# Weight loads of a hybrid-heads network's projections, issued from ScalarE's queue instead of SyncE's

## The chip, the cores and the metric

The kernel runs on one core of a Trainium2 chip. The metric is the device time of one execution in microseconds (us), lower is better. An engine executes its own instructions in the order in which they stand in the program; SyncE (SP) does nothing but issue transfers and wait.

## The reference, cut to what matters

Two layers of a network work on 512 latent and 256 context tokens of 2048 channels, all in 32-bit floats. Each layer modulates the normalised input, applies one large input projection, feeds four kinds of heads (a diagonal state space model "S5", windowed attention, bidirectional RWKV-7, Hyena convolutions), gates their outputs and applies an output projection:

```python
for l in range(DEPTH):                       # DEPTH = 2, D_MODEL = 2048
    mod_x = silu(c) @ w_ada[l] + b_ada[l]    # shift, scale, gate; the same for the context
    hx = rms_norm(x, norm_g[l]) * (1.0 + scale_x) + shift_x
    s5u, q, k, v, rkv, lora, hy, g = split_proj(hx @ w_in[l])
    y = concat(rms_norm(s5(s5u)), rms_norm(attention(q, k, v)), rwkv(rkv, lora), rms_norm(hyena(hy)))
    x = x + gate_x * ((y * silu(g)) @ w_out[l])
```

The context runs through the same weights; after the second layer only the latent tokens are wanted.

## The kernel before

Tiles have 128 partitions (channels) and up to 768 tokens (512 latent, 256 context). The input projection of a layer has 51 output tiles of 128 channels; each is computed in four parts (`kq` in `inprojs`, L1621), and a part uses one weight tile `wr` of 128x512 (256 KB). That is 408 loads from `in_win` over both layers. The output projection (`outproj`, L1716) has 16 output tiles with four such parts, 128 loads from `in_wo`.

A weight tile goes through three steps. `raw` (L1477) gives one of `WRB` = 3 buffers `wr`, and SyncE issues the load (L1629 or L1725). `split` (L1480) makes two parts of it: ScalarE (ACT) copies it to the rounded type, `wh` (L1484), and VectorE (DVE), or GpSimd (POOL) for every fourth part, subtracts that from the original, `wl` (L1485). `WHB` = 2 buffers of `wh` and `wl` exist. TensorE (PE) then multiplies: 12 matmuls of 512 columns and, where the context is wanted, 12 of 256 for each part (L1645, L1735). A buffer `wr` is free again when `wh` and `wl` have been made; a buffer `wh` when the part's matmuls are done.

Beside the input projection runs the modulation of later use: 64 blocks of `w_ada` (`ada_block`), four loads each (L1540, issued by SyncE) into the same three `wr` buffers, each read by four small matmuls (L1542). While these blocks run (to 2730 us), loads of `in_win` and of `in_wada` take the three buffers in turn. A few other loads (L248, L256, L1028) use them too.

The heads run at the same time as the projection. The one that matters below is RWKV: 24 groups of chunks, 12 in each layer, each of which goes round features (VectorE), an inversion on GpSimd (L398, L399: 62 instructions), with transfers ahead of it (`rwAd`, `rwAb`) and behind it (`rwXd` L401, `rwXP` L402), and a chain of small matmuls with ScalarE and VectorE between them (L439 to L466; `rwKU`, L448, is ScalarE's link). S5 loads 512 small tables (`s5T`, L807). All transfers of the kernel, 2575, are issued by SyncE.

A scheduler lays down the order of every engine when the kernel is built: it takes instructions by priority as they become ready on its own clock. `prio(WP)` gives loads and splits a priority 2000 instructions ahead of their place. At run time nothing is reordered: an instruction whose data are late holds all that stand behind it on its engine.

Of the kernel before, what the change touches and what calls it, by code (L numbers as in the profile page):

```python
# [37 lines left out]
# columns of the packed RWKV parameters  # L38
# [15 lines left out]
def pack_rw(I):  # L54
    f = [cols(I["rw_mu_prev"]), cols(I["rw_mu_next"]), cols(I["rw_w0"].reshape(2, -1)), cols(I["rw_a0"].reshape(2, -1)),
         cols(I["rw_k_k"]), cols(I["rw_k_a"]), cols(I["rw_r_k"].reshape(2, -1)), cols(I["rw_ln_g"]), cols(I["rw_ln_b"])]
    p = np.concatenate(f, axis=2)
    for o in (RP["mup"], RP["mun"]):
        p[:, :, o + 12] = p[:, LORA_ORDER, o + 12]
    wa = np.stack([I["rw_w2"], I["rw_a2"]], axis=2)  # layer, direction, (w, a), row, output  # L60
    return {"rwp": p, "rwwa": np.ascontiguousarray(wa.reshape(2, 4, 32, 512))}


class K:
# [26 lines left out]
    def padded(self, lat, ctx):  # L91
        """Copies a projection tile beside zeros; its used width with the last zero excluded."""
# [8 lines left out]
    @contextmanager  # L101
    def prio(self, offset):
        """Work that goes before what was traced up to offset instructions earlier."""
        self.tc.cur_priority -= offset
        yield
        self.tc.cur_priority += offset
# [9 lines left out]
    def ring(self, shape=(128, 512)):  # L116
        """The banks beside those of the input projection, in turn."""
# [3 lines left out]
    def rms(self, y, sq, tmp, eng, eps, gate=None):  # L121
        """1 / sqrt(mean square + eps) over 4 channel tiles y, in sq (all of one width). With gate, which runs beside it: half of that, from 4 eps."""
# [19 lines left out]
class Pace:  # L142
    """Issue order on the tensor engine: units of a filling stream issue behind steps of a leading one."""
# [4 lines left out]
    def step(self, ins, allow):  # L148
        """ins leads; the units that come before it grow by allow."""
        self.n += allow  # L150
        self.steps.append((self.n, ins.ins.name))
# [18 lines left out]
class RwFeed:  # L170
    """Token shift of the RWKV projections; r, k, kk, v and the half logits kept in both orders of time."""

    def __init__(self, k, l, raw):
# [5 lines left out]
        # 1 - mu_prev - mu_next, w0 / 2, a0 / 2, k_a / 2, 1 - k_a, 2 - k_a  # L179
# [11 lines left out]
        # r, k, kk, v and tanh of the half logits (decay, a), forward and reversed  # L191
# [7 lines left out]
    def store(self, d, z, ctx):  # L199
        """z [128, 769] (latent | - | context) into d [128, 2, NT], as it is and reversed."""  # L200
# [8 lines left out]
    def feed(self, j, lat, ctx):  # L209
        """Projection tile j (r 0-3, k 4-7, v 8-11, lora 12) in lat / ctx [128, n]: token shift."""  # L210
# [30 lines left out]
    def logits(self, lz):  # L241
        """tanh of half the decay and a logits of all channels: (high, low, high, low) x (high, high, low, low) in one product. In 8 parts."""
# [30 lines left out]
class Rwkv:  # L273
    """Bidirectional RWKV-7 over chunks of 64 steps; both directions advance together, each in its own order of time."""
# [13 lines left out]
    def features(self, c, g):  # L288
        """Scores and transposed operands of 4 chunks of two heads."""
# [6 lines left out]
        S = t([128, 2, 4, 2, 128], "rwS", self.nbuf)  # direction, (pair, head), parity  # L296
        KU = t([128, 2, 2, 2, 2, 128], "rwKU", self.nbuf)  # direction, pair, parity, (K/B | V/U)
# [28 lines left out]
        # slots of a pair: K even | B even | B odd | K odd, in the place of k and kk  # L326
# [17 lines left out]
        # end-scaled K (natural), B (chunks of a pair exchanged)  # L344
# [25 lines left out]
    def rows(self, b):  # L370
        """Partitions of the B rows and of the K rows of chunks of parity b."""
# [5 lines left out]
    def invert(self, S, XT):  # L377
        """Transposed inverses of the unit triangular scores; column 4 m + g of matrix u on partition 4 u + g."""
# [10 lines left out]
        grp = [(b, q, self.rows(b)[0].start + 32 * q) for b in (1, 0) for q in range(2)]  # by rising row  # L389
# [13 lines left out]
        # natural order of the columns; a row block is used from its diagonal on  # L403
# [3 lines left out]
        # off-diagonal block of the inverse: -X1^T A21^T X2^T  # L407
# [81 lines left out]
    def finish(self, c, Y, n0, out):  # L489
        """Head norm and bonus of the tokens from n0 on, in Y."""  # L490
# [5 lines left out]
        for a in range(n0, n0 + n, 256):  # L496
# [5 lines left out]
            # bonus: r k (2 - k_a + k_a (a forward + a backward)) summed over a head  # L502
# [73 lines left out]
def pack_s5(I):  # L576
    def st(a):  # [L,2,G,P] -> [L,128,2*G] with both halves alike
# [4 lines left out]
    lam = np.stack([st(I["s5_lam_re"]), st(I["s5_lam_im"]), stp], axis=2)  # [L,128,3,64]  # L582

    def bt(a):  # [L,2,G,P,H] -> [L,P,2G,H]
# [5 lines left out]
    bs = np.stack([np.concatenate([br, bi], 1), np.concatenate([bi, br], 1)], axis=2)  # [L,128,2,64,16]  # L590
# [7 lines left out]
class S5:  # L598
    """Bidirectional diagonal state space model over chunks of 8 tokens."""
# [7 lines left out]
    def turns(self, out, x, tmp, eng):  # L607
        """out = x - round(x)"""
# [3 lines left out]
    def prepare(self):  # L612
# [33 lines left out]
        # turns per chunk  # L646
# [6 lines left out]
        # powers 0..8 of lambda  # L653
# [18 lines left out]
        # (lambda - 1) / lam  # L672
# [15 lines left out]
        # BA = [re; im], BB = [-im; re] of the discretised input matrix  # L688
# [11 lines left out]
        # CA = [cr; -ci], CB = [-ci; -cr]  # L700
# [15 lines left out]
    def tile(self, ct, src):  # L716
        """Channel tile ct (8 groups); src [128, 768] in DRAM."""
# [6 lines left out]
        Uc = t([96, 8, 8, 16], "s5Uc")  # chunk | group, 7 - s, h  # L724
# [7 lines left out]
        U = t([128, 8, 128], "s5U")  # (7 - s, h) | group, chunks ctx, lat, ctx  # L732
# [6 lines left out]
        Yc = t([96, 8, 8, 16], "s5Uc")  # chunk | t, group, o  # L739
# [12 lines left out]
    def batch(self, g0, U, Yc):  # L752
        """Two groups, both directions."""
# [4 lines left out]
        def dg(a):  # [128, 64, ..] -> [128, 2, 2, ..]  # L758
# [7 lines left out]
        for d in range(2):  # L766
# [7 lines left out]
            # outputs at step t: forward lambda^(t+1), backward lambda^(8-t)  # L774
# [13 lines left out]
        # impulse response within a chunk: K_j[o, h] with h on partitions  # L788
# [20 lines left out]
        # drive matrices with (7 - s, h) on partitions: re | im | re  # L809
# [7 lines left out]
        # rotation tables  # L817
# [11 lines left out]
        # drives, rotated: v cos + [im; -re] sin  # L829
# [9 lines left out]
        # x: sin with the sign of [+; -]  # L839
# [6 lines left out]
        # rotated back, one chunk later, chunks in natural order lat | ctx  # L846
# [21 lines left out]
    def glu(self, outs, bg, eps):  # L868
        """Gated linear unit, then the branch norm."""
# [45 lines left out]
def hy_const(ns=(512, 256)):  # L915
    c = {}
    f = np.float32
    for n in ns:
# [6 lines left out]
        # taps: even, then odd  # L925
        h = n // 2
        ms = np.arange(n).reshape(h // 128, 128, 2).transpose(1, 2, 0)  # [128, parity, tile]
        c[f"hydec{n}"] = np.exp(-t * deltas[None, :]).astype(f)[ms].reshape(128, n // 128, 512).copy()
        # frequencies k below n / 2 (even, then odd) carry those of n - 1 - k too
# [7 lines left out]
        # [128 taps, frequency tile, cos / sin, parity, tap tile, 128]  # L937
        c[f"hykt{n}"] = kt.reshape(128, 2, 2, h // 128, h // 128, 128).transpose(0, 4, 1, 2, 3, 5).astype(f).copy()
        od = base % 2 == 1
        kk = np.concatenate([np.where(od, n - 1 - base, base), np.where(od, base, n - 1 - base)])  # even, then odd  # L940
        w = np.pi * (kk + 0.5) / n
        tau = np.arange(h)[:, None] + 0.5
        p, q = np.cos(tau * w) + np.sin(tau * w), np.cos(tau * w) - np.sin(tau * w)  # [h, n]
        # forward: a -> P even, b -> M even, b -> P odd, a -> M odd
        fw = np.stack([p[:, :h], q[:, :h], p[:, h:], q[:, h:]])  # [4, h, h]
        c[f"hyfw{n}"] = fw.reshape(4, h // 128, 128, h).transpose(2, 0, 1, 3).astype(f).copy()  # [128 t, 4, tt, k]
        c[f"hyiv{n}"] = fw.transpose(0, 2, 1).reshape(4, h // 128, 128, h).transpose(2, 0, 1, 3).astype(f).copy()  # [128 k, 4, kt, t]
# [18 lines left out]
class HyFilter:  # L966
    """Spectra of the filters. raw, split: buffers of 2 KB and their split."""
# [12 lines left out]
    def angle(self, ps, b, f, n):  # L980
        """f (ps + b) brought to the range of the sine."""
# [10 lines left out]
    def hidden(self, l, n):  # L992
        """The two layers with sines, transposed: high parts over low parts."""
# [24 lines left out]
    def tables(self, n):  # L1018
# [4 lines left out]
        self.tb = [t([128, 2, 2, 4, 128], f"hftb{i}", 1, F32R) for i in range(2)]  # frequency tile, cos / sin, (parity, taps)  # L1023
# [8 lines left out]
    def spectra(self, l, f, out):  # L1032
        """In 4 parts; appends the spectra of both orders to out."""
# [3 lines left out]
        for o in range(2):  # L1037
            # frequency tiles even then odd; [cos, sin] spectra scaled by 1 / (2 n)
# [7 lines left out]
            for s in (1, 0):  # L1046
# [4 lines left out]
                for par in range(2):  # L1051
                    S = []
                    for mt in range(h):
# [6 lines left out]
                        if par + mt == 0:  # L1060
                            # the backward filter has no tap at 0: half of sum and difference
# [29 lines left out]
class HyFeed:  # L1091
    """Convolution over 3 tokens of the projections."""
# [7 lines left out]
    def feed(self, j, lat, ctx):  # L1100
        """Projection tile j (v 0-3, x1 4-7, x2 8-11): convolution over 3 tokens."""
# [10 lines left out]
class Hyena:  # L1112
# [8 lines left out]
    def seq(self, n0, n, G):  # L1121
# [11 lines left out]
        for o in range(2):  # L1133
            # folded inputs, time on partitions
# [11 lines left out]
            # spectra P, M; products  # L1146
# [20 lines left out]
            for c in range(4):  # L1167
# [3 lines left out]
                # even P and odd M are even about the middle, the others odd  # L1171
# [16 lines left out]
    def finish(self, gates, bg, eps, put):  # L1188
        """Branch norm and gates; put takes the tiles."""
# [18 lines left out]
def att_const():  # L1208
# [5 lines left out]
    pm = np.zeros((128, 128), f)  # [source, destination]  # L1214
# [20 lines left out]
class KvFeed:  # L1235
    """RMS norm of queries and keys over heads of 64 channels."""
# [6 lines left out]
    def feed(self, gi, dram, lat, ctx):  # L1243
        """One tile of queries (gi 0) or keys (1)."""
# [16 lines left out]
class Attn:  # L1261
    """Windowed grouped-query attention with sinks; latent and context queries."""
# [16 lines left out]
    def rotate(self, x):  # L1279
        """Rotary embedding of the latent tokens."""  # L1280
# [8 lines left out]
    def run(self, srcs, pool):  # L1289
        """srcs: q 0-3, k, v. The results stay in pool."""  # L1290
# [6 lines left out]
        # keys of a group, both halves alike: high and low parts  # L1297
# [19 lines left out]
        def load(c):  # L1317
# [4 lines left out]
            # first head: high over low parts; second head: low over high parts  # L1322
# [25 lines left out]
    def finish(self, gates, outs, bg):  # L1348
        """Branch norm and gates."""
# [597 lines left out]
```

## Time and profile before

| | |
|---|---|
| Time, median of 3 runs | 3715.77 us (3714.04 to 3724.52) |
| Span of the profiled execution | 3742.2 us; no separate time of that execution is given |
| Profiled span against the median | 26.4 us or 0.7% longer |
| PE busy | 3482.5 us, 93% of the span |
| DVE, ACT, POOL busy | 60%, 40%, 37% |
| Granted TensorE clock, mean | 0.952 of full speed |
| Bytes moved by transfers | 515.12 MB, 138 GB/s over the span |

The profile's rows are of one execution. A wait row says which instruction waited for which, the total in us, how often and the longest. "Busy" leaves out issuing and waiting; so all of SyncE is waiting or issuing, and a wait there costs something only if what stands behind it is wanted sooner.

### The profile page before, as it was taken

To read this page: it belongs to the slowest core of one execution; us is meant where nothing else is said; L and a number is where in the kernel's file an instruction comes from. 1 tells how busy PE (TensorE), PEld (TensorE's weight loads), DVE (VectorE), ACT (ScalarE), POOL (GpSimd) and SP (SyncE) were. 2 spreads that over 40 slices of the span, in tenths; PEclk is the share of its full clock that TensorE was granted. 3 is DMA by queue.
4 is the path that set the end of the run, shared out by engine and by line. 5 is a ranking of instruction groups with operands and counts; after the bars stand their busy time and mean duration, and the time that the engine had idled before them with its cause. 6 is when DMAs were issued, how large, how long until landed. Compare 5 with 4: busy or idle time off the path is not lost. (4 is left out here: it accounts for less than half of the span.)

```text
span 3742.2 us, 63165 instructions
## 1 busy us (share of the span) xinstructions
PE 3482.5 (93%) x23222; PEld 2692.6 (72%) x23222; DVE 2234.8 (60%) x4239; ACT 1491.1 (40%) x2875; POOL 1386.2 (37%) x2508
## 2 busy tenths in 40 slices
PE   5897899999999999999999978999999999999999
PEld 1465777777778777788777866776776767677867
DVE  7673666546555544366667664775466565546765
ACT  3344433434344433244313454443434443435522
POOL 5642664152435242000143424663434455411031
PEclk9998999999999999999999988999988998999999
DMA  7855344554445444543633325435533433435244
GB/s 241 273 174 157 106 115 126 174 159 112 138 133 144 134 135 132 160 129 113 216 113 101 111 86 151 130 102 170 171 89 109 123 99 112 120 119 185 66 158 121
DMA packets 546737, 515.12 MB, mean 138 GB/s; under 512 B 166425, under 2 KB 392506, under 8 KB 545532
## 3 DMA queue, kind: packets, MB, share of 16 engines
q1 hardware_dynamic: 546428, 511.08, 45.2%
q8 instruction: 184, 3.01, 0.3%
q14 instruction: 125, 1.02, 0.1%
HBM read 406.59 MB, written 100.93 MB: 136 GB/s over the span
## 5 line engine op out<-in xcount | busy, mean ns | idle before, releaser
L1645 PE MATMUL pin<-hxh,wh 128*128 128x512 f32 (+1 forms) x2624 | 988.9, 377 | 10.6 <-ACT ev L267 5.0
L1645 PE MATMUL pin<-hxh,wl 128*128 128x512 f32 (+1 forms) x2624 | 946.2, 363 | 13.7 <-POOL wl L1485 10.0
L1645 PE MATMUL pin<-hxl,wh 128*128 128x512 f32 (+1 forms) x2624 | 945.8, 361 | 0.0
L1484 ACT ACTIVATE wh<-wr 128x512 fp32r<-128x512 f32 x548 | 344.4, 629 | 828.3 <-PE pin L1645 389.5
L1645 PEld LDWEIGHTS pin<-hxh,wh 128*128 128x128 f32 x2624 | 506.7, 193 | 126.7 <-issue 32.3
L1645 PEld LDWEIGHTS pin<-hxh,wl 128*128 128x128 f32 x2624 | 505.5, 193 | 96.1 <-POOL wl L1485 12.9
L1645 PEld LDWEIGHTS pin<-hxl,wh 128*128 128x128 f32 x2624 | 508.1, 194 | 73.3 <-issue 5.3
L1485 DVE TENSOR_TENSOR wl<-wr,wh 128x512 fp32r<-128x512 f32 x434 | 318.6, 734 | 306.7 <-ACT wh L1484 290.1
L1485 POOL TENSOR_TENSOR wl<-wr,wh 128x512 fp32r<-128x512 f32 x114 | 159.0, 1395 | 868.9 <-ACT wh L1484 755.5
L398 POOL TENSOR_TENSOR rwtm<-rwAb,rwX 128x60 f32<-128x60 f32 (+24 forms) x744 | 258.2, 347 | 343.9 <-DMA rwAb<-rwAd 148.1
L1735 PE MATMUL pin<-yh,wl 128*128 128x512 f32 (+1 forms) x768 | 281.5, 368 | 6.5 <-DVE wl L1485 6.4
L1735 PE MATMUL pin<-yh,wh 128*128 128x512 f32 (+1 forms) x768 | 281.8, 368 | 3.5 <-ACT yh L1711 1.3
L399 POOL TENSOR_TENSOR rwX<-rwX,rwtm 128x60 f32<-128x60 f32 (+24 forms) x744 | 263.1, 354 | 57.4
L1735 PE MATMUL pin<-yl,wh 128*128 128x512 f32 (+1 forms) x768 | 280.5, 365 | 2.3 <-DVE yl L1712 2.0
L1735 PEld LDWEIGHTS pin<-yh,wl 128*128 128x128 f32 x768 | 145.9, 190 | 32.3 <-DVE wl L1485 9.7
L1735 PEld LDWEIGHTS pin<-yh,wh 128*128 128x128 f32 x768 | 145.9, 190 | 30.1 <-ACT yh L1711 3.8
L1735 PEld LDWEIGHTS pin<-yl,wh 128*128 128x128 f32 x768 | 146.2, 190 | 26.7 <-DVE yl L1712 3.4
L1739 DVE SCALAR_TENSOR_TENSOR xt<-pin,GT,xt 128x512 f32<-128x512 f32 (+1 forms) x144 | 93.8, 656 | 87.0 <-PE pin L1735 86.7
L1542 PE MATMUL pin<-wr,cs 128*32 128x128 f32 x2048 | 119.8, 290 | 15.5 <-DMA wr<-in_wada 11.7
L448 ACT ACTIVATE rwKU<-mU 64x256 f32<-64x256 f32 x96 | 36.2, 377 | 194.4 <-PE mU L446 193.4
L466 DVE TENSOR_TENSOR rwst<-rwst,mU 64x128 f32<-64x128 f32 x160 | 45.3, 283 | 87.4 <-PE mU L459 84.6
L340 PE MATMUL mA<-rwZR,rwld 64*128 64x128 f32 x768 | 91.7, 288 | 5.5 <-DVE rwS L342 4.5
(608 smaller groups left out, 6548.7 us busy)
## 6 DMA issues: line engine op xcount, KB each, us to landing
wr<-in_win SPq DMA_DIRECT2D x408, 256.0 KB
wr<-in_wada SPq DMA_DIRECT2D x256, 256.0 KB
ada<-in_wada SPq DMA_DIRECT2D x64, 512.0 KB
wr<-in_wo SPq DMA_DIRECT2D x128, 256.0 KB
rwld<-rwF SPq DMA_DIRECT2D x20, 1024.0 KB
rwF<-ev SPq DMA_DIRECT2D x64, 256.0 KB
xt<-in_xin SPq DMA_DIRECT2D x32, 384.0 KB
rwLA<-ev SPq DMA_DIRECT2D x32, 384.0 KB
```

What stands on the lines that cost most here:

```text
L340: nc.tensor.matmul(pss[:, p, b, :], kb[hr, d * 2 + p, 2 * b:2 * b + 2, :].rearrange("p b s -> p (b s)"), ZR[hr, d, :, tt * 64:tt * 64 + 64 ...
L398: E.tensor_tensor(tm, Ab[:, 0:s, s:s + 1].to_broadcast([128, s, w]), X[:, s:s + 1, m:8].to_broadcast([128, s, w]), ALU.mult)
L399: E.tensor_tensor(X[:, 0:s, m:8], X[:, 0:s, m:8], tm, ALU.subtract)
L448: nc.scalar.activation(KU[rB, :, p, b, 1, :], up[rB].rearrange("p d a b -> p d (a b)"), AF.Copy, scale=-1.0)
L466: V.tensor_tensor(new[hs, :, hs], new[hs, :, hs], sp[hs], ALU.add)
L1484: nc.scalar.activation(h, raw, AF.Copy)
L1485: (nc.gpsimd if i % 4 == 3 else nc.vector).tensor_tensor(l, raw, h.bitcast(F32), ALU.subtract)
L1542: nc.tensor.matmul(ps[32 * j:32 * j + 32, :], self.cs[:, q * 4 + j, :], w3[:, j], start=q == 0, stop=q == 3, tile_position=(0, 32 * j))
L1645: mm.append(nc.tensor.matmul(ps, w[:, c], x[:, t], start=a, stop=b))
L1735: nc.tensor.matmul(ps, w[:, c], y[:, t], start=a, stop=b)
L1739: nc.vector.scalar_tensor_tensor(x[:, t], ps, self.GT[l][:, s, j:j + 1], x[:, t], ALU.mult, ALU.add)
```

## The change

A new method issues the weight loads of both projections from ScalarE's queue. Each load is given an order (without a semaphore, within ScalarE's own queue) behind the split of the part two before it. All other transfers, those of the modulation's blocks among them, stay with SyncE. Comments were taken out as well, and lines behind them move by up to 9: the split's L1484 and L1485 become L1493 and L1494, the loads' L1629 and L1725 become one line, L1484, the modulation's L1540 becomes L1549.

```diff
         self.pace = None
+        self.whs = []
...
+    def load(self, src):
+
+        r = self.raw()
+        i = self.nc.scalar.dma_start(out=r, in_=src).ins
+        if len(self.whs) >= 2:
+            self.tc.add_manual_dep(i, self.whs[-2], mybir.DependencyInfo(mybir.DependencyClass.NoSync, mybir.DependencyReason.DATA), reason="load")
+        return r
+
     def split(self, raw, i=0, pool=None):
...
-        nc.scalar.activation(h, raw, AF.Copy)
+        self.whs.append(nc.scalar.activation(h, raw, AF.Copy).ins.name)
...
                 with self.k.prio(WP):
-                    r = self.raw()
-                    nc.sync.dma_start(out=r, in_=self.ins["win"][l, j, :, kq])
+                    r = self.load(self.ins["win"][l, j, :, kq])
                     W.append(self.split(r, kq))
...
                 with self.k.prio(WP):
-                    r = self.raw()
-                    nc.sync.dma_start(out=r, in_=self.ins["wo"][l, j, :, q])
+                    r = self.load(self.ins["wo"][l, j, :, q])
                     h, lo = self.split(r, iq)
```

In the order that is built, SyncE has 2039 transfers instead of 2575 and ScalarE 536. Of these 536, 352 stand directly behind a split in ScalarE's order, and 200 stand behind the split of the part just before theirs, not two before. The places at which the prediction looks are these.

SyncE in layer 1, RWKV's third group there. `wr` are weight tiles, `rwXd` the result of the inversion. Before:

```order
L305 DMA rwla_27739<-rwLA_21482 128x4x256
L114 DMA qkv_21923<-ev_31372 128x256
L1629 DMA wr_31466<-in_win 128x512
L1629 DMA wr_31484<-in_win 128x512
L1629 DMA wr_31502<-in_win 128x512
L1629 DMA wr_31520<-in_win 128x512
L1629 DMA wr_31549<-in_win 128x512
L401 DMA rwXd_27487<-rwX_27489 32x32x8 x4
L402 DMA rwXP_27490<-rwXd_27487 128x256
```

Now:

```order
L305 DMA rwla_27739<-rwLA_21482 128x4x256
L114 DMA qkv_21923<-ev_31372 128x256
L401 DMA rwXd_27487<-rwX_27489 32x32x8 x4
L402 DMA rwXP_27490<-rwXd_27487 128x256
L393 DMA rwX_27841<-in_rwunit 128x256
```

The five weight loads that stood ahead of `rwXd` are gone from this queue.

ScalarE in layer 1 at the same group. Before:

```order
L1484 ACTIVATE wh_31468<-wr_31466 128x512
L317 ACTIVATE rwla_27739<-rwL_27742 128x512
L323 ACTIVATE rwL_27742<-rwla_27739,rwd_21467,rwp_21465 128x512
L1484 ACTIVATE wh_31486<-wr_31484 128x512
L1251 ACTIVATE ev_31456<-pin_31382 128x512
L1255 ACT_TABLE_LOAD
L1255 ACTIVATE ev_31456<-pin_31459,epsn 128x512
L1484 ACTIVATE wh_31504<-wr_31502 128x512
```

Now:

```order
L1493 ACTIVATE wh_31468<-wr_31466 128x512
L317 ACTIVATE rwla_27739<-rwL_27742 128x512
L1484 DMA wr_31502<-in_win 128x512
L323 ACTIVATE rwL_27742<-rwla_27739,rwd_21467,rwp_21465 128x512
L1493 ACTIVATE wh_31486<-wr_31484 128x512
L1484 DMA wr_31520<-in_win 128x512
L1251 ACTIVATE ev_31456<-pin_31382 128x512
L1255 ACT_TABLE_LOAD
L1255 ACTIVATE ev_31456<-pin_31459,epsn 128x512
L1493 ACTIVATE wh_31504<-wr_31502 128x512
```

Each load stands behind a split, with one more split between it and its own (`wr_31502` is loaded behind the split of `wr_31466`, and split behind that of `wr_31484`).

ScalarE in layer 0, while a modulation block runs beside the projection (`adg` and `ev` empty PSUM banks of the finished tile, `rwKU` is RWKV's link). Before:

```order
L424 ACTIVATE rwXT_1510_7066<-mI_11479 32x8x32 x2
L448 ACTIVATE rwKU_11240<-mU_11503 64x2x128
L1484 ACTIVATE wh_17305<-wr_17303 128x512
L1546 ACTIVATE adg_17294<-pin_17135 128x128
L1696 ACTIVATE ev_17282<-pin_17136 128x512
L1484 ACTIVATE wh_17341<-wr_17339 128x512
L1696 ACTIVATE ev_17282<-pin_17137 128x256
L448 ACTIVATE rwKU_11240<-mU_11528 64x2x128
```

Now:

```order
L424 ACTIVATE rwXT_1510_7066<-mI_11479 32x8x32 x2
L1484 DMA wr_17303<-in_win 128x512
L448 ACTIVATE rwKU_11240<-mU_11503 64x2x128
L1493 ACTIVATE wh_17305<-wr_17303 128x512
L1484 DMA wr_17339<-in_win 128x512
L1555 ACTIVATE adg_17294<-pin_17135 128x128
L1704 ACTIVATE ev_17282<-pin_17136 128x512
L1493 ACTIVATE wh_17341<-wr_17339 128x512
L1704 ACTIVATE ev_17282<-pin_17137 128x256
L1484 DMA wr_17375<-in_win 128x512
L1484 DMA wr_17411<-in_win 128x512
L448 ACTIVATE rwKU_11240<-mU_11528 64x2x128
```

The loads now stand ahead of `rwKU`, `adg` and `ev`, and only one or two instructions ahead of their own splits.

## Rows read from the trace of the kernel before

**Rows 1.** The page's head and busy time: us, share of the span, instructions.
```profile
span 3742.2 us, 63165 instructions
...
PE 3482.5 (93%) x23222; PEld 2692.6 (72%) x23222; DVE 2234.8 (60%) x4239; ACT 1491.1 (40%) x2875; POOL 1386.2 (37%) x2508
```

**Rows 2.** Windows by stage: length, busy us (instructions) by engine, clock, DMA share, GB/s.
```profile
300.00:700.00 400.00, 359.72 (x2332) 289.08 (x2334) 233.38 (x473) 170.92 (x314) 190.79 (x305) 0.93 0.42 121
700.00:1550.00 850.00, 829.79 (x7014) 666.64 (x7015) 450.69 (x894) 325.54 (x641) 303.46 (x792) 0.98 0.48 140
...
2160.00:2610.00 450.00, 399.87 (x2528) 320.21 (x2526) 284.45 (x541) 200.86 (x374) 213.08 (x317) 0.93 0.42 124
2610.00:3320.00 710.00, 664.81 (x4775) 495.52 (x4776) 394.11 (x781) 288.39 (x560) 308.05 (x784) 0.91 0.41 119
```

**Rows 3.** Waits of PE for weight parts: us in total, times, longest.
```profile
PE pin L1645 <- POOL wl L1485: 10.0, 7, 3.4
...
PE pin L1735 <- DVE wl L1485: 6.4, 5, 2.1
...
PE pin L1645 <- ACT wh L1484: 4.3, 6, 1.4
...
PE pin L1645 <- DVE wl L1485: 3.6, 3, 1.8
...
PE mI L1645 <- DVE wl L1485: 2.6, 1, 2.6
...
PE mI L1645 <- ACT wh L1484: 1.5, 2, 1.0
```

**Rows 4.** Waits of ACT for weight tiles, the same columns.
```profile
ACT wh L1484 <- PE pin L1645: 389.5, 194, 7.3
...
ACT wh L1484 <- DMA wr<-in_win: 132.6, 46, 8.3
```

**Rows 5.** Waits of SyncE's queue at the weight loads, the same columns.
```profile
SPq L1629 <- DVE wl L1485: 300.6, 91, 26.8
SPq L1629 <- PE pin L1542: 232.1, 91, 11.5
SPq L1725 <- DVE wl L1485: 221.9, 92, 8.6
...
SPq L1629 <- POOL wl L1485: 88.8, 23, 8.1
```

**Rows 6.** Issues of both lines: count, duration ns min/median/max, first and last start.
```profile
L1629 SPq DMA_DIRECT2D wr<-in_win x408: 327/334/1985, 114.3 to 3410.3; - x136
L1725 SPq DMA_DIRECT2D wr<-in_wo x128: 327/328/648, 1762.1 to 3725.9; - x128
```

**Rows 7.** Timeline of SyncE, then POOL's last row of that inversion: start, us.
```profile
2757.15 33.29 SPq L1629 DMA_DIRECT2D wr<-in_win  x5
2790.53 3.08 SPq L401 DMA_DIRECT2D rwXd<-rwX  x4
...
2782.60 0.20 POOL L399 TENSOR_TENSOR rwX<-rwX,rwtm 128x8 f32<-128x8 f32 x1
```

**Rows 8.** Windows, columns as in rows 2, from inversion's end to its use, four groups.
```profile
2731.00:2752.00 21.00, 21.00 (x202) 17.69 (x199) 11.13 (x23) 8.56 (x19) 1.27 (x1) 1.00 0.37 76
2783.00:2798.00 15.00, 14.93 (x65) 11.20 (x65) 12.57 (x18) 6.83 (x10) 1.42 (x1) 0.87 0.29 55
2840.00:2854.00 14.00, 14.00 (x73) 11.01 (x71) 12.77 (x16) 6.20 (x9) 1.30 (x1) 0.95 0.43 91
2956.00:2983.00 27.00, 27.00 (x212) 21.43 (x209) 16.35 (x31) 15.71 (x30) 1.63 (x3) 1.00 0.43 105
```

**Rows 9.** The split on ACT: counts, ns min/median/max; ACTq is ACT's sequencer.
```profile
L1484 ACT ACTIVATE wh<-wr x548: 611/631/681, 48.5 to 3732.7; 128x512 fp32r<-128x512 f32 x183
L1484 ACTq EVENT_SEMAPHORE  x529: 17/38/7791, 60.2 to 3729.9; - x177
```

**Rows 10.** Chain of waits: start, us, what; transfers of weights on it, 2600 to 2900.
```profile
2613.62 5.45 DMA wr<-in_win
...
2867.77 2.39 DMA wr<-in_win
```

**Rows 11.** ACT's timeline in the last stage; in brackets the idle time ahead.
```profile
3701.88 0.63 ACT L1484 ACTIVATE wh<-wr 128x512 fp32r<-128x512 f32 x1 [2.17 <-PE pin L1735]
3704.68 0.63 ACT L1484 ACTIVATE wh<-wr 128x512 fp32r<-128x512 f32 x1 [2.17 <-PE pin L1735]
```

## Prediction, made before the changed kernel was run

> **What bounds the kernel now.** I read the page's busy times first, then windows by stage, then who waits for a weight tile on the way from its load to the matmul (PE, ACT, SyncE), then single places on the timeline.
>
> PE is busy 93% of the span and ACT 40% [rows 1]. By stage the slack differs [rows 2]: in layer 0's RWKV stage (700 to 1550 us) PE idles 850.00 - 829.79 = 20 us, 2%; in layer 1's (2610 to 3320) 45 us, 6%, at a mean clock of 0.91; in the two stretches of S5 (300 to 700, 2160 to 2610) 40 and 50 us, about 10%. So PE's fixed order with few gaps sets the time. A change off PE can give back some of these gaps or add to them, and nothing else.
>
> What late weights cost now is seen in three steps. PE's own waits for a split part make 10.0 + 6.4 + 4.3 + 3.6 + 2.6 + 1.5 = 28.4 us [rows 3]. ACT's split waited 132.6 us, 46 times, for a tile's transfer, but 389.5 us for PE to give a `wh` buffer back [rows 4]: mostly the tile is there first. SyncE stood at the load for 300.6 + 88.8 us until the subtraction of an earlier tile had freed the buffer, and 232.1 us until a modulation block's matmuls (L1542) had [rows 5]. These waits are not SyncE's doing: the three buffers stay as they are.
>
> **The change, part by part.**
>
> *Off SyncE: 536 issues of 0.33 us* [rows 6], 179 us of its queue, and the waits at them. What stood behind comes sooner. The clearest case is in RWKV of layer 1: the inversion ends at 2782.60 + 0.20 = 2782.80 us, and its result leaves at 2790.53, because five weight loads stood in SyncE's queue ahead of it [rows 7]: 7.7 us late. By the same two timelines three other groups are 2.3, 5.0 and 4.0 us late; the order of instructions shows the cause gone. But from the inversion's end to the first use PE was busy 76.93 of 77.00 us in these four windows [rows 8]: other matmuls that stand ahead in its order cover the lateness. Worth 0.07 us at most in these windows, so 0. Were this cover gone (less projection beside RWKV), the 19 us would count in full. For small transfers elsewhere, S5's tables above all, I take 2 us.
>
> *Loads that reach ACT sooner.* All 28.4 us of PE's waits [rows 3] are the upper bound, 0 the lower. A load that waited for its buffer is not issued sooner from another queue, and the waits at the buffers (300.6, 232.1, 88.8) are several times the 132.6 us that ACT waited. I take a third: -9 us.
>
> *On ACT: the issues.* No row shows an issue on ACT; SyncE's 0.33 us is the nearest [rows 6]. 352 of the 536 stand directly behind a split, which occupies ACT's datapath for 0.63 us [rows 9]; there I count nothing. The other 184 x 0.33 = 61 us stand in ACT's queue. To turn ACT's lateness into PE's, I use what rows give: 28.4 / 132.6 = 0.21 if all PE waits for parts came from late tiles, (4.3 + 1.5) / 132.6 = 0.04 if only those that name ACT did. I take 0.1: +6 us; bounds 0 and 61 x 0.21 = 13.
>
> The sequencer of ACT, like SyncE's, waits by instructions of its own: 529 of them around 548 splits, up to 7.79 us long [rows 9]. The Trainium skill (Perfetto Trace Analysis, section "DVE / Act Engine Instruction") says that an engine instruction is pushed into a wait queue and the sequencer goes on to the next. By that rule the load would go out while earlier ACT work still waits, the 6 us would fall to 0 and the sum by 6. By the row the sequencer itself stands still ahead of nearly every split, and I keep the 6.
>
> *On ACT: the waits.* A load whose buffer isn't free now stops ACT, with the rest of ACT's work queued behind it: the emptying of PSUM banks (`adg`, `ev`), and RWKV's link `rwKU`, for which PE waits next. Outside the modulation stretch the pin takes care of it: the subtraction that frees the buffer belongs to a part before the split that the load stands behind, so I count 0 for the 300.6 and 221.9 us. In the modulation stretch the buffer is that of a modulation block and the pin says nothing of it: up to 232.1 us in 91 waits [rows 5] move to ACT. ACT comes to the load later than SyncE did (200 loads stand one split later than their pin), so most of each wait is over; I take a fifth, 46 us, and at 0.1: +5 us. Bounds: 0, and 232.1 x 0.21 = 49.
>
> *Is a pinned load early enough?* Two parts lie between the split it follows and its own. The shortest parts are in the last stage, 2.80 us each (3704.68 - 3701.88) [rows 11], so 5.6 us; less the split (0.63) and the issue (0.33) that leaves 4.6 us for a transfer. Pieces of such transfers on the chain take 2.39 to 5.45 us [rows 10]. So typically in time, at worst 0.8 us late for ACT, and PE has the other `wh` buffer then. 0.
>
> Sum: -2 - 9 + 6 + 5 = 0 us on the profiled span of 3742.2. That span is 26.4 us above the median of the runs, 3715.77; as the sum is a difference I put it on the median: **3716 us**.
>
> **The rivals.** A measurement of this kernel tells about 0.3%, 11 us, from no change.
>
> *SyncE was the brake* (faster). All of PE's 28.4 us of waits for parts go, ACT pays nothing: 3716 - 28 = 3688. If the 19 us of late inversions show up as well (the stage has 45 us of gaps, and its clock of 0.91 would rise with fewer of them), 3669. For: seven to eight us of one queue's delay on a loop that is nothing but latency, in four groups of twelve. Against: PE without a gap in just these windows [rows 8].
>
> *ACT's queue stops* (slower). The wait for the modulation's matmuls, 232.1 us at 91 loads, comes to stand on ACT whole and is passed on at 0.21: +49; with the issues' upper bound of 13: 3716 + 62 = 3778. The place is 300 to 1550 and 2160 to 2730 us; half of it gives 3747. It decides from where ACT is held 11 / 0.21 = 52 us longer than now, that is if a quarter of the waits move. For: in the new order loads stand ahead of `rwKU`, `adg` and `ev` there, and one or two instructions ahead of their own split, so that ACT also sits out the transfer. Against: ACT idles 60% of the span, and PE idles 2% in layer 0's RWKV stage, so chains there have room.
>
> *The pin does not bite.* It orders, it doesn't advance: in the modulation stretch the buffers decide when a load can go, from whichever queue. Then nothing changes but the order around it: within 11 us of 3716. This shares the forecast's outcome.
>
> **How the numbers follow.** No measurable change (the forecast, and the pin that doesn't bite): 0.42. Faster: 0.30, as the lateness on SyncE is certain and its cover may be thinner than one execution shows, also because PE's order moves a little all over. Slower: 0.28, as a stop of ACT reaches everything that empties PSUM. The faster case runs from 3669 to 3704, the slower from 3727 to 3778; the range cuts each near its middle, which leaves about 2 in 10 out: 3684 to 3754. The forecast's own range is 3705 to 3727.
>
> **What would show it.** If right: SyncE's waits at L1629 are gone, `rwXd` leaves within a microsecond of the inversion's end in all groups of layer 1, PE's busy share in those windows is as now, its waits for `wh` and `wl` stay within 10 us of 28, ACT's busy time stays at 1491 us, and its idle time ahead of `rwKU`, `adg` and `ev` hardly grows. Wrong on the fast side: PE's gaps from 2610 to 3320 fall well below 45 us and the clock there rises above 0.91. Wrong on the slow side: PE's gaps from 300 to 1550 grow, ended by ACT's emptying of banks or `rwKU`, with a load ahead of them in ACT's queue that waits for L1542.

## The result: slower by 2.3%, and the profile after

The changed kernel takes 3804.38 us in the median of four runs (3799.97 to 3817.34), the kernel before beside it 3720.14 (3714.04 to 3729.47). The ratio is 1.023, with a 95% interval of 1.0206 to 1.0255: 84 us slower, outside the predicted range, whose upper end was 3754.

The page's head and its busy times, as in [rows 1]:

```profile
span 3806.7 us, 63245 instructions
...
PE 3492.4 (92%) x23222; PEld 2706.0 (71%) x23222; DVE 2219.3 (58%) x4239; ACT 1493.4 (39%) x2876; POOL 1395.1 (37%) x2508
```

The engines execute the same instructions but for one more on ACT; ACT is busy for 2 us more, PE for 10. PE's waits for split parts, as in [rows 3], then ACT's waits for tiles, as in [rows 4], and SyncE's at the modulation's loads, which it still issues:

```profile
PE pin L1653 <- DVE wl L1494: 11.6, 7, 3.8
...
PE pin L1742 <- DVE wl L1494: 5.9, 6, 2.9
...
PE mI L1653 <- DVE wl L1494: 2.8, 2, 1.4
...
PE pin L1653 <- POOL wl L1494: 2.3, 3, 1.1
...
PE pin L1653 <- ACT wh L1493: 2.1, 3, 0.9
...
PE mI L1653 <- ACT wh L1493: 0.4, 1, 0.4
```

```profile
ACT wh L1493 <- PE pin L1653: 444.1, 212, 10.2
...
ACT wh L1493 <- DMA wr<-in_win: 65.4, 28, 5.3
```

```profile
SPq L1549 <- DVE wl L1494: 238.8, 74, 14.5
...
SPq L1549 <- PE pin L1551: 150.3, 45, 12.6
```

PE's waits for parts sum to 25.1 us (28.4 before) and ACT's for a transfer are halved (132.6 before). So loads do reach ACT sooner, and it is worth 3 us to PE. SyncE still waits hundreds of us for the same three buffers, now at the modulation's loads. The new issues on ACT's sequencer, and the waits that go with them:

```profile
L1484 ACTq DMA_DIRECT2D wr<-in_win x408: 334/334/1337, 113.9 to 3477.1; - x136
L1484 ACTq EVENT_SEMAPHORE  x385: 17/17/4972, 112.6 to 3757.9; - x193
L1484 ACTq DMA_DIRECT2D wr<-in_wo x128: 334/334/368, 1801.2 to 3791.6; - x128
```

An issue takes the 0.33 us that was assumed, and the median wait at a load is 17 ns; all 385 together are 17.5 us. ACT is not stopped there.

Where the time is lost shows when the same split (matched by its tile) is looked up in both traces:

| start before, us | 699.9 | 1506.3 | 2341.0 | 2537.4 | 2703.2 | 3226.4 | 3689.8 |
|---|---|---|---|---|---|---|---|
| later after, us | -15.3 | 42.3 | 47.0 | 50.6 | 81.5 | 72.1 | 64.4 |

Layer 0's RWKV loses 58 us, and layer 1's passage from S5 to RWKV (2537 to 2703) another 31. The execution of before that these are set against was itself a long one: it ends 33 us later than that of dummy_issues (below), which has the same order and the same loads. Against that one the changed kernel is only 7 us ahead at 700 us, loses 59 in layer 0's RWKV and 30 in that passage, and wins nothing back behind 2703. Windows between the same two splits, before, then after; the columns are those of [rows 2]:

```profile
771.00:1506.00 735.00, 718.14 (x6256) 575.48 (x6255) 389.19 (x789) 283.70 (x565) 285.34 (x764) 0.98 0.47 133
...
2537.00:2703.00 166.00, 152.47 (x981) 116.59 (x979) 86.26 (x143) 59.52 (x108) 51.13 (x101) 0.97 0.54 166
```

```profile
763.00:1548.60 785.60, 746.62 (x6281) 599.35 (x6279) 395.69 (x809) 290.25 (x581) 298.81 (x770) 0.94 0.45 126
...
2588.00:2784.70 196.70, 164.93 (x1090) 125.12 (x1089) 87.62 (x152) 66.98 (x120) 58.79 (x124) 0.91 0.50 150
```

In layer 0's stage PE's gaps grow from 17 to 39 us, and about the same matmuls take 28 us longer at a mean granted clock of 0.94 instead of 0.98. Among PE's waits there the one for the inversion's result has grown. It stood at 3.7 us in 2 waits in this stage, and is now:

```profile
PE mI L415 <- DVE rwXP L411: 21.0, 8, 5.0
```

### The profile page after: what moved, and what is told of

The parts are those of the page before. It is cut to its first block, busy times and chain, and to the rows that moved or that the text cites. A ratio compares the mean times of both kernels' runs of the same rounds, so it can differ in the third digit from the quotient of the medians.

```text
span 3806.7 us, 63245 instructions
## 1 busy us (share of the span) xinstructions
PE 3492.4 (92%) x23222; PEld 2706.0 (71%) x23222; DVE 2219.3 (58%) x4239; ACT 1493.4 (39%) x2876; POOL 1395.1 (37%) x2508
## 5 line engine op out<-in xcount | busy, mean ns | idle before, releaser
L1653 PE MATMUL pin<-hxh,wl 128*128 128x512 f32 (+1 forms) x2624 | 944.1, 363 | 14.1 <-DVE wl L1494 11.6
L1493 ACT ACTIVATE wh<-wr 128x512 fp32r<-128x512 f32 x548 | 343.7, 629 | 771.5 <-PE pin L1653 444.1
L1653 PEld LDWEIGHTS pin<-hxh,wh 128*128 128x128 f32 x2624 | 508.3, 194 | 127.0 <-issue 32.5
L1494 DVE TENSOR_TENSOR wl<-wr,wh 128x512 fp32r<-128x512 f32 x434 | 319.3, 736 | 265.7 <-ACT wh L1493 246.7
L1494 POOL TENSOR_TENSOR wl<-wr,wh 128x512 fp32r<-128x512 f32 x114 | 157.2, 1380 | 824.1 <-ACT wh L1493 713.9
L398 POOL TENSOR_TENSOR rwtm<-rwAb,rwX 128x60 f32<-128x60 f32 (+24 forms) x744 | 257.4, 346 | 403.0 <-DMA rwAb<-rwAd 220.2
L399 POOL TENSOR_TENSOR rwX<-rwX,rwtm 128x60 f32<-128x60 f32 (+24 forms) x744 | 271.1, 364 | 57.3
L1742 PEld LDWEIGHTS pin<-yl,wh 128*128 128x128 f32 x768 | 146.2, 190 | 27.6 <-POOL yl L1720 3.6
L1746 DVE SCALAR_TENSOR_TENSOR xt<-pin,GT,xt 128x512 f32<-128x512 f32 (+1 forms) x144 | 93.5, 655 | 80.1 <-PE pin L1742 79.8
L405 ACT ACTIVATE rwXT<-rwXP 32x256 f32<-32x256 f32 x96 | 64.2, 669 | 113.0 <-DMA rwXP<-rwXd 111.5
L770 POOL TENSOR_TENSOR s5B<-s5BA,s5PR 128x256 f32<-128x256 f32 x64 | 63.4, 1012 | 117.0 <-PE mA L814 102.4
```

The costliest lines, as they stand in the source:

```text
L398: E.tensor_tensor(tm, Ab[:, 0:s, s:s + 1].to_broadcast([128, s, w]), X[:, s:s + 1, m:8].to_broadcast([128, s, w]), ALU.mult)
L399: E.tensor_tensor(X[:, 0:s, m:8], X[:, 0:s, m:8], tm, ALU.subtract)
L405: nc.scalar.activation(XT[r:r + 32, :, 32 * q:32 * q + 32].rearrange("p u (m g) -> p u m g", g=4), XR[r:r + 32].rearrange("p u (g m) -> p ...
L770: G.tensor_tensor(o, X[:, d].unsqueeze(2).to_broadcast(sh), pr, ALU.mult)
L1493: self.whs.append(nc.scalar.activation(h, raw, AF.Copy).ins.name)
L1494: (nc.gpsimd if i % 4 == 3 else nc.vector).tensor_tensor(l, raw, h.bitcast(F32), ALU.subtract)
```

## Experiments: the order or the queue?

The edit moves loads to another queue. It also makes the scheduler lay another order on every engine: 9723 of PE's 17629 matmuls stand at another place in its order, 2228 of VectorE's 4239 instructions. The kernel before was run again beside each set of experiments and took 3711.92, 3715.05 and 3723.38 us there, so versions are compared by their ratios to it. The two effects can be taken apart, since instructions have the same numbers in both kernels. A table of these numbers, added at the end, ties each instruction to the one ahead of it on its engine (all but the weight loads):

```diff
         build(tc, args, res)
+        force(nc, tc)
...
+def force(nc, tc):
...
+        for p, q in zip(names, names[1:]):
+            tc.add_manual_dep(by[q], p, mybir.DependencyInfo(mybir.DependencyClass.NoSync, mybir.DependencyReason.DATA), reason="order")
```

**order_before**: the changed kernel with the table of the kernel before.

> The loads stay on ScalarE's queue as in the changed kernel, but the other instructions of all five engines are held to the order that they had in the kernel before. Theory A (order): the 86 us come from the new order that the scheduler laid down on every engine once the loads counted as ScalarE's work, and issuing from ScalarE itself costs or gains little; then this runs at 3720 +/- 15 us, with PE's waits at L415 for the inversion back near 4 us in layer 0. Theory B (queue): they come from what happens at run time, weight transfers side by side with RWKV's small ones and ScalarE held at its loads; then this runs at 3785 to 3825 us. In between, the split of the 86 us between the two can be read off.

Measured: 3760.31 us against 3711.92, ratio 1.0109 (1.0069 to 1.0149), five runs from 3732.89 to 3785.67. Neither theory alone: PE's wait at L415 is back at 4.2 us, as theory A has it, but issuing from ACT's queue costs some 40 us by itself, with a wide spread.

**order_after**: the kernel before with the table of the changed one.

> The mirror image: all loads on SyncE's queue as before, but the other instructions of all five engines held to the order of the changed kernel. Theory A (order): slow, 3785 to 3825 us, with SyncE issuing everything. Theory B (queue): 3720 +/- 15 us.

Measured: 3781.96 us against 3711.92, ratio 1.0176 (1.0155 to 1.0197), 3 us below theory A's range. Without one load on ACT, three quarters of the loss are there. Its trace repeats the changed kernel's course: PE's wait at L415 stands at 17.3 us, and against dummy_issues it loses 48 us in layer 0's RWKV and 29 in layer 1's passage. The two parts sum to 2.85%, more than the 2.3% of both together; the excess is hardly beyond the intervals.

**pin_on_sync**: the changed kernel with the issue back on SyncE, and the scheduler's own order.

```diff
-        i = self.nc.scalar.dma_start(out=r, in_=src).ins
+        i = self.nc.sync.dma_start(out=r, in_=src).ins
```

> The pin alone: every load gets the order behind its split of two parts before, but all stay on SyncE's queue; the scheduler lays its own order, which differs from that of before in fewer places than the changed kernel's. If the pin is what makes the order worse: 3750 us or more. If it is that the loads count as ScalarE's work: 3700 to 3730 us.

Measured: 3717.92 us against 3723.38, ratio 0.9979 (0.995 to 1.0008): no difference. The pin alone doesn't make the bad order (3278 matmuls stand elsewhere than before); it takes the loads to count as ACT's work. Loads on ACT without the pin weren't run.

## Experiments: where the order costs

A table may also follow one kernel's order up to a time of its trace and the other's from there, as what had started by then is complete in itself. All loads are on SyncE in this section.

**handover_before**: the table of before up to 800 us, then that of the changed kernel.

> All loads on SyncE; every engine follows the order of the kernel before up to 800 us of its trace (the end of layer 0's S5 and the start of RWKV's first two groups), and from there the order of the changed kernel. With the changed order all through, this was 3782 us against 3712. Theory A1 (the place is the hand-over from S5 to RWKV: PE waits 9.6 us at L235 and takes projection matmuls between the first group's L340, so that RWKV's loop starts 20 us late and its 12 groups, a chain of latencies, end late): about 20 us of the 70 go, 3752 to 3768 us. Theory A2 (the loss is spread over RWKV's groups, in which the new order is worse everywhere): 3775 to 3790 us.

Measured: 3773.18 us against 3715.05, ratio 1.0166 (1.0139 to 1.0194). Theory A1 falls. RWKV starts as early as before (the first group's L340 ends at 744.4 us, 769.0 in order_after), but the lead is gone by group 2 (counted from 0), whose inversion starts at 896 us, 891 in order_after. From the end of L340 in group 2 to that in group 11 it still takes 565.9 us (568.4 in order_after), where the order of before takes 541.9 (tail_after, below). The loss is in the loop. Step by step over these ten groups, order_after against tail_after: GpSimd's inversions 286.5 instead of 270.1 us, the way from VectorE's scores to them 89.4 instead of 79.8, the way back to ACT 81.2 instead of 77.4.

Why would GpSimd's own instructions be slower in another order? GpSimd and VectorE in one inversion of order_after, on the timeline:

```profile
1299.15 0.27 POOL L398 TENSOR_TENSOR rwtm<-rwAb,rwX 128x42 f32<-128x42 f32 x1
1299.50 0.75 POOL L399 TENSOR_TENSOR rwX<-rwX,rwtm 128x42 f32<-128x42 f32 x1
...
1301.65 0.56 POOL L398 TENSOR_TENSOR rwtm<-rwAb,rwX 128x28 f32<-128x28 f32 x1
1302.29 0.57 POOL L399 TENSOR_TENSOR rwX<-rwX,rwtm 128x28 f32<-128x28 f32 x1
1302.94 0.23 POOL L398 TENSOR_TENSOR rwtm<-rwAb,rwX 128x24 f32<-128x24 f32 x1
```

```profile
1298.97 0.43 DVE L441 TENSOR_TENSOR rwBV<-mU,rwBV 64x256 f32<-64x256 f32 x1
1299.43 0.69 DVE L1485 TENSOR_TENSOR wl<-wr,wh 128x512 fp32r<-128x512 f32 x1
1300.04 0.76 DVE L331 TENSOR_TENSOR rwld<-rwla 128x512 f32<-128x512 f32 x1
1300.72 0.73 DVE L332 TENSOR_TENSOR rwld<-rwL,rwla 128x512 f32<-128x512 f32 x1
1301.38 0.74 DVE L346 TENSOR_TENSOR rwla<-rwld,rwPC 128x512 f32<-128x512 f32 x1
1302.04 0.72 DVE L345 TENSOR_TENSOR rwL<-rwld,rwPC 128x512 f32<-128x512 f32 x1
```

L398 multiplies and L399 subtracts; at 128x42 elements either takes 0.27 us wherever no VectorE instruction runs beside it in this trace. Here L398 takes 0.27 beside L441, which has one input in PSUM, and L399 takes 0.75 beside L1485, which has both in SBUF. 128x28 elements take 0.56 and 0.57 beside L346 and L345 (0.24 alone), and the next instruction, 128x24, is down to 0.23. The new order puts the next group's L319 to L332, L345 and L346 inside the inversion, 29 of them in these ten groups; in tail_after there is none. The Trainium skill (SBUF — State Buffer, section "🔬 SBUF: two separate sides") says that VectorE and GpSimd lock one port pair for a whole instruction where a VectorE instruction has two inputs in SBUF; these rows agree (0.75 us instead of 0.27).

**features_behind**: order_after, with 21 of VectorE's entries in the table put behind the inversion's end.

> The run with the changed order and all loads on SyncE (3782 us), with one thing altered: in four groups of layer 0's RWKV (the trace's groups 2, 4, 8 and 10, counted from 0) 21 VectorE instructions of the next group (L319 to L332, L345, L346; 0.7 us each) that stood inside GpSimd's inversion go behind its end. Theory D1 (GpSimd's multiplications run longer while VectorE's two-input instructions run): the four inversions took 26.5 + 29.6 + 30.5 + 28.1 = 114.7 us and come down to 103 to 108; the time falls by that or less, 3770 to 3783 us. Theory D2 (the inversions are longer for another reason): they stay at 112 to 117 us, 3775 to 3790 us.

Measured: 3764.32 us against 3723.38, ratio 1.0095 (1.0058 to 1.0132), below both theories' ranges. The four inversions take 25.5 + 27.6 + 27.4 + 26.7 = 107.2 us: D1. Group 6, in which eight such instructions stay inside, keeps its length (30.5 us, 30.6 in order_after, 26.9 in tail_after). For the one at 1274 us, GpSimd's 31 products of L398 (windows of that line alone: length, busy, clock, DMA share, GB/s), in order_after and here:

```profile
1274.10:1304.64 30.54, 11.99 (x31) 1.00 0.42 135
```

```profile
1276.37:1303.81 27.44, 10.17 (x31) 0.94 0.47 147
```

The time fell by more than the 7.5 us of these inversions. By the traces 7 us of it come in layer 0 (groups 2 to 11 take 557.8 us instead of 568.4); the rest shows up behind 2900 us, where nothing was altered and runs of one order also differ, so it isn't claimed.

**l1_handover_before**: the changed order, but layer 1's passage from S5 to RWKV in the order of before.

> All loads on SyncE, the changed order up to 2480 us of its own trace, then what the kernel before had done by 2745 us in the order of before, then the changed order again: only layer 1's hand-over from S5 to RWKV gets its old order back. With the changed order all through, 35 us were lost between 2440 and 2680 us. Theory E1 (that place by itself): 3745 to 3758 us. Theory E2 (the loss only becomes visible there, and comes from work left undone earlier): 3772 to 3785 us.

Measured: 3754.92 us against 3723.38, ratio 1.0089 (1.0062 to 1.0117). Theory E1: about 30 us are lost in this one place. What it is can be read in the changed kernel's own trace, first VectorE, then ACT, then PE:

```profile
2649.54 1.02 DVE L215 SCALAR_TENSOR_TENSOR ev<-zp,rwp,ev 128x769 f32<-128x769 f32 x1 [0.49 <-ACT ev L214]
2651.53 3.35 DVE L136 RECIPROCAL s5T<-s5T 128x512 f32<-128x512 f32 x1 [0.98 <-ACT s5T L135]
2654.80 0.92 DVE L216 SCALAR_TENSOR_TENSOR ev<-zp,rwp,ev 128x769 f32<-128x769 f32 x1
```

```profile
2655.76 0.94 ACT L232 ACTIVATE ev<-ev,rwp 128x769 f32<-128x769 f32 x1 [4.26 <-DVE ev L216]
```

```profile
2647.55 1.02 PE L134 MATMUL mU<-s5T,c_ones 128*128 128x512 f32 x2
2656.75 2.93 PE L235 MATMUL pin<-ev,c_blk 128*128 128x512 f32 x4 [8.18 <-ACT ev L232]
```

RWKV's token shift (L215, L216, L232) feeds L235. The new order lets S5's reciprocal, 3.35 us, in between L215 and L216, and puts L235 on PE just behind S5's last sum (L134), with no projection matmuls between. PE stands for 8.18 us; 120 us earlier it stands for 10.36 behind an earlier L232. Together that is 18.5 of the some 30 us; the rest stands in the windows above as 12 us more busy time of PE, with 1090 matmuls in them instead of 981 and a granted clock of 0.91 instead of 0.97, and wasn't taken apart. In order_after both waits are the same to 0.03 us (8.19 and 10.33). In the order of before L216 follows L215 directly, L136 comes eleven instructions later, and no such wait is seen.

**tail_after**: the table of before up to 2745 us, then that of the changed kernel.

> All loads on SyncE; the order of the kernel before up to 2745 us of its trace (layer 1's hand-over to RWKV included), and from there the order of the changed kernel. With the changed order all through, the time lost shrank by 20 to 25 us behind 2692 us. If that order is better by itself in layer 1's RWKV: 3685 to 3700 us. If the shrinking was only a late start being made up: 3705 to 3720 us.

Measured: 3697.83 us against 3715.05, ratio 0.9962 (0.9947 to 0.9977). The order that the edit brought is better than the old one in one stretch, and this version is 0.4% (some 14 us) below the kernel before and some 100 us below the changed one, with no load on ACT.

**best_of_both**: as tail_after, and the changed order up to 640 us as well.

> All loads on SyncE; the changed order up to 640 us (S5 of layer 0 runs 14 to 25 us ahead there), then the order of the kernel before up to 2745 us, then the changed order again. If a gain made in S5 is kept when the hand-over's order is the one of before: 3665 to 3695 us. If the stages' ends are set by work that S5's lead does not bring forward: within 10 us of the run with only the tail changed.

Measured: 3700.25 us against 3715.05, ratio 0.996 (0.9938 to 0.9982): within 10 us of tail_after. But it says little of S5's lead, which was read against the long execution of before. The last matmul of that S5 (L862) starts at 640.0 us here, at 637.9 in tail_after, at 643.7 in dummy_issues and at 650.3 in that execution: beside other executions of the old order there is hardly a lead to keep.

## Experiments: what the queue costs

**dummy_issues**: the kernel before with its own order and loads, and idle transfers on ACT.

```diff
+    scr = nc.dram_tensor("scr", (536, 128), F32, kind="Internal").ap()
+    dummy = [nc.scalar.dma_start(out=scr[j:j + 1], in_=src[0, 0, 0:1, 0, 0:128]).ins.name for j in range(536)]
```

> The kernel before in its own order with all its loads on SyncE, and 536 extra transfers of 512 bytes into an unused piece of DRAM, issued by ScalarE at the places where the loads stand when the order of before is kept (that run took 48 us more than before). Nothing reads them. Theory B1 (ScalarE's 0.33 us for each issue lengthen the chains that run through it): 3735 to 3770 us. Theory B2 (the 48 us come from where and when the 256 KB transfers themselves run): 3705 to 3725 us.

Measured: 3716.34 us against 3715.05, ratio 1.0014 (0.9996 to 1.0033): nothing that can be measured, though these issues are longer than a load's:

```profile
L1955 ACTq DMA_DIRECT2D scr<-in_win x536: 495/496/891, 113.5 to 3693.8; - x179
```

536 x 0.495 = 265 us of ACT's sequencer are free here. Theory B1 falls.

**tail_after_act**: tail_after, every instruction in the same order, with the loads outside the modulation's stretch on ACT.

```diff
-    def load(self, src):
+    def load(self, src, sync=False):
...
-        i = self.nc.scalar.dma_start(out=r, in_=src).ins
-        if len(self.whs) >= 2:
+        i = (self.nc.sync if sync else self.nc.scalar).dma_start(out=r, in_=src).ins
+        if not sync and len(self.whs) >= 2:
...
-                    r = self.load(self.ins["win"][l, j, :, kq])
+                    r = self.load(self.ins["win"][l, j, :, kq], part)
```

> The order of the run with only the tail changed (3698 us, all loads on SyncE), with one thing altered: the 280 loads for which no modulation block runs beside the part are issued by ScalarE with the pin, as in the changed kernel. No order differs, and the modulation's stretch is untouched. Theory B2 (weight transfers that run beside RWKV's small ones lengthen its loop): 3708 to 3730 us, with the last step of L401's transfers 5 us or more longer over layer 1's groups. Theory F (the prediction's rival: SyncE is the brake in layer 1, and relieving it counts): 3675 to 3695 us. Neither: within 5 us of 3698.

Measured: 3737.89 us against 3723.38, ratio 1.0035 (1.0017 to 1.0053), where tail_after had 0.9962. So the queue alone costs 0.7%, some 27 us, and theory F falls. Theory B2's sign is there (the flights of L401, below), though the time is 8 us above its range. Of the 33 us between the two traces 25 come behind 2690 us, in the very stretch where relieving SyncE was to count. No instruction's order differs, issues as such cost nothing measurable (dummy_issues), and ACT stands at these loads for 2.3 us in all. What is left is the transfers themselves. Layer 1's groups 13 to 23 take 546.4 us instead of 523.5; this pair alone wouldn't show it, as the order of before, loads on SyncE, took 546.6 in one execution and 527.8 in another. What waits for transfers in that stretch: SyncE at the read back of the result (L402) and of the scores (L392) for the write ahead of each, and GpSimd for its input; in tail_after, then here:

```profile
SPq L402 <- DMA rwXd<-rwX: 17.7, 15, 2.0
SPq L392 <- DMA rwAd<-rwS: 7.5, 7, 2.5
...
POOL rwtm L398 <- DMA rwAb<-rwAd: 53.9, 6, 15.9
```

```profile
SPq L402 <- DMA rwXd<-rwX: 30.6, 19, 4.1
SPq L392 <- DMA rwAd<-rwS: 18.0, 10, 2.9
...
POOL rwtm L398 <- DMA rwAb<-rwAd: 74.0, 8, 14.4
```

All of GpSimd's waits at L398 in that stretch, whatever they are put down to, sum to 89.5 and 101.2 us. The issues are in time; it is the flights that are longer. From the end of the last of L401's four issues to the last landing, summed over the eleven groups, it is 35.7 us instead of 27.4, for L391 22.7 instead of 15.4, together 15.6 us of the groups' 22.9. The nine traces here with these loads on SyncE have 26.4 to 28.3 and 14.1 to 17.5 there, the five with them on ACT 32.5 to 36.6 and 17.8 to 23.9. (For the two transfers read back, L402 and L392, the two sets of traces overlap.) A weight load was under way beside these steps with one queue too, but for less of them: 16.3 of the 27.4 us and 2.1 of the 15.4, against 22.8 of 35.7 and 13.8 of 22.7 from two queues. And a step of L401 with a load beside it took 2.2 to 3.6 us there and 2.4 to 4.1 here, where those without one took 2.2 and 2.5. That they share the same DMA engines then, as the Trainium skill says (DMA: Bandwidth & Descriptors, section "Issuing engines are not separate DMA queues"), fits these times; how they share them wasn't measured.

**act_after_mod**: the same edit with the scheduler's own order.

> Loads of in_win stay with SyncE, without a pin, as long as a modulation block runs beside the part, and go to ScalarE with the pin only where none does (from about 2730 us on), as do all of in_wo. Both theories put the loss at 700 to 1500 and 2540 to 2720 us, ahead of that point, so both expect the loss gone: 3690 to 3725 us. If the 15 us that the changed kernel won back after 2720 us are due to ScalarE's queue, 3700 to 3710. A time above 3760 would say that the loss is not in the modulation stretch.

Measured: 3739.3 us against 3711.92, ratio 1.0063 (1.0038 to 1.0088). The loss in the modulation's stretch is gone, as both theories had it, and still it isn't as fast as before: 14 us above the expected range. That fits the queue's price behind 2730 us, which the run above shows by itself; here the scheduler's order differs too.

**all_on_act**: the changed kernel with the modulation's loads on ACT too.

```diff
-            nc.sync.dma_start(out=w3, in_=w4[q])
+            nc.scalar.dma_start(out=w3, in_=w4[q])
```

> The modulation's loads into the same three buffers go to ScalarE too, so that no load into wr of the projection's stretch stands in SyncE's queue. Theory C (SyncE still stands at the modulation's loads, 538 us at L1549 in the changed kernel, with RWKV's transfers behind them): most of the loss goes, 3720 to 3750 us. Theory B: no better, 3790 to 3850, as all weight transfers still run beside the small ones and ScalarE has 256 more waits. Theory A: a third order, with a time that none of the others tells, within 2% of either.

Measured: 3778.22 us against 3711.92, ratio 1.0174 (1.0142 to 1.0206). Theory C, that SyncE's waits at the modulation's loads make the loss, falls: none of them is left, and three quarters of the loss are. As the order is a third one, it decides nothing between the other two.

## Why the prediction was wrong

- **Right, and worth little**: an issue on ACT takes 0.33 us; ACT's busy time is the same; ACT stands at its loads for 17.5 us, where the "+5" took 46 (whether the pin is the reason wasn't tested); tiles reach ACT sooner. The -9 us for PE's waits for parts came out as -3.
- **Mis-sized**: "+6" for issues on ACT. Five hundred longer ones cost nothing measurable (interval -0.04% to 0.33%). The row by which it was kept shows the sequencer waiting ahead of nearly every split, but for a median of 38 ns [rows 9]: at half of them it hardly stands still.
- **The step that failed** is the premise that "PE's fixed order with few gaps sets the time" and that a change off PE can only give back gaps or add to them. The change gave PE another order: more than half of its matmuls stand elsewhere, which can be read from the two orders without any run. So the sum, -2 -9 +6 +5, has no term for the order of the other instructions. The prediction saw that it moves ("a little all over", on the fast side; "within 11 us" where the pin doesn't bite) but gave no reason for so small a price. It is the largest term: 1.76%, some 65 us, with no load moved. Some 30 of them are shown to stand in layer 1's passage. In layer 0's RWKV, VectorE's instructions inside four of GpSimd's inversions account for 7; the rest there was located but not taken apart.
- **The second**: "What stood behind comes sooner", worth 0 to 2 us. The small transfers were then longer in flight beside the weight loads: 0.7% for the 280 loads outside the modulation's stretch alone.
- **The slow rival** had a time near the measured one (3747 to 3778) by the wrong mechanism, so that is luck: ACT's queue doesn't stop. The place that it named, 300 to 1550 and 2160 to 2730 us, is where the loss is, but by the order.
- **The cover** of [rows 8] may have been thinner than thought. `rwXd` left 19 us late in all in layer 1 in the profile of before, and 5 us late in that of dummy_issues, which has the same order; groups 13 to 23 took 546.6 and 527.8 us. Two executions don't settle it. The sign that `rwXd` would leave within a microsecond everywhere in layer 1 failed too: in the changed kernel two groups are 2.5 and 4.5 us late, the first behind a modulation load at which SyncE stood.

## What to carry to other kernels

Where a scheduler lays the order down, a change of the issuing engine is a change of the whole program: compare the orders first, look at the places where the bounding engine changes hands between stages, and hold the order fixed to learn what the edit itself is worth. A queue with many small, latency-bound transfers wasn't relieved here by moving large loads to another queue, as both were then in flight together for longer. And an order found by accident can be kept in parts: the best version here takes 0.4% off with no load moved.

## What the runs showed of the hardware that was not expected

- GpSimd's two-input instructions can take two to three times as long beside VectorE's with two inputs in SBUF (0.75 us against 0.27 for 128x42 elements). With 29 of the latter inside, ten inversions took 16 us longer.
- 536 extra issues of 0.495 us on ACT's sequencer cost nothing measurable on a kernel whose ACT is busy 40% of the span.
- Executions of one and the same order differ: five of order_before spread over 53 us, ten of tail_after_act over 18, and 24 of the kernel before over 35. What sets the spread wasn't looked into.
